# Branch products, output projection, second norm and the first up-projection steps written into one fixed order with the mLSTM

## The chip, the core and the metric

The kernel runs on one core of one Trainium2 chip. Its time is the device time of one execution in microseconds; a kernel is run several times and the median is taken. A profile is one more execution, with the hardware profiler on.

## What is computed

One layer of a diffusion backbone over 1024 tokens of width 1024, with 256 context tokens before them. All arithmetic has the accuracy of float32.

```
h   = modulate(rms_norm(x), sh1, sc1)               # six modulation rows from c
q, k, v, mq, mk, mv, mo, mg, ga, gm = split(h @ w_in)
att = windowed_gqa(q, k, v, context keys)           # 16 heads, window 128
ml  = mlstm_readout(mlstm_bidirectional(mq, mk, mv, mg), mo)
y   = sigmoid(ga) * (att @ w_branch_att) + sigmoid(gm) * (ml @ w_branch_ml)
x   = x + g1 * (y @ w_out)
u   = modulate(rms_norm(x), sh2, sc2) @ w_up        # 1024 -> 2 x 2816
out = x + g2 * ((silu(conv(u)_g) * conv(u)_a) @ w_down)
```

## The kernel before

**Products.** TensorE multiplies float32 operands as two parts: a high part, rounded on ScalarE (`copy_act`, L44), and a low part, the remainder, from VectorE (L49). One step of a product is three matmuls, high by high, low by high and high by low (`mm3`, L90 to L92; `product`, L1901 to L1903); most have 512 columns. A 1024 x 1024 x 1024 product is 16 tiles (one PSUM bank each) of 8 steps, 384 matmuls.

**Stages.** After the start come attention (about 90 to 645 us of the profile), the mLSTM (to about 1005), `stage_tail` (to about 1320) and `stage_ffn`. In attention and in the mLSTM every instruction of TensorE, VectorE, ScalarE and GpSimd is pinned behind the one before it on its engine (class `Pinned`, L494; all of these have line L504 in the trace). Their order is a string in which each letter is one small step: `ORDER` is run through once for each of the blocks of 128 tokens, `ORDER_GATES` and `ORDER_CORE` once. In `stage_tail` nothing is pinned: the program states the steps, and a scheduler places them on the engines.

**Around the change.** The last part of `ORDER_CORE` holds the first half of the attention branch product (letters N load, X high, Z low, Y step, l gate; tiles `ya`, operands `a0`, `a1`, `a2`, each 512 wide). Their buffers lie over the normalised input `hT`, which is closed when the mLSTM's output gate (`mo`) no longer needs it. `stage_tail` then has the second half of that product (`ya` on `wba1`), the mLSTM branch (`ym` on `mT`, `wbm0`, `wbm1`), the output projection (`op` on `y`, `wo0`, `wo1`), the second norm with its transposes (`x2t`), and the up projection, a product in fast form (seven products of half the size in place of eight): operands `b11`, `b21`, `t1` to `t4`, `b22` come from sums of quarters, and the weight sums of the down projection lie between projection tiles. The transposes of the pair sums (`x2p`) are stated between the last projection tiles.

**Modulation.** A modulation row of 512 is eight products on VectorE (`mod_product`, tiles `wmb` and `macc`) and then eight one-column matmuls over two rows (`mod_row`); `g1` and `g2` are transposed (`gT`) and stored. Products 0 to 47 are in attention (letter p of `ORDER`), 48 to 63 in the mLSTM branch of the tail, with three buffers.

**Memory and queues.** PSUM has 8 banks of 512 columns: two for products (`mm`), one (`fl`), three for transposes (`tp`) and two that attention uses for scores, the mLSTM for states (`d`) and the up projection afterwards. Each pool hands out its banks as they come free. Stored gates `sga_d`, `sgm_d` and first branch results `y1_d` are loaded over ScalarE's DMA queue (`ahead`), four tiles ahead; everything else is on SP's queue.

Of the kernel before, what the change touches and what calls it, by code (L numbers as in the profile page):

```python
# [99 lines left out]
def layer_kernel(ctx: ExitStack, tc: tile.TileContext, A: dict, out: bass.AP, dbg=None):  # L100
# [25 lines left out]
    ps1 = psx.enter_context(tc.tile_pool(name="ps_mm", bufs=2, space=PSUM, reuse_waits="tile"))  # L126
    pst = psx.enter_context(tc.tile_pool(name="ps_tp", bufs=3, space=PSUM, reuse_waits="tile"))
# [10 lines left out]
    def mm_tile(name):  # L138
        return ps1.tile([P, 512], F32, tag="mm", name=name)

    def fl_tile(name):
        return ps1.tile([P, 512], F32, tag="fl", name=name, bufs=1)

    def tp_tile(name):
        return pst.tile([P, 512], F32, tag="tp", name=name)

    def s_tile(name):
# [6 lines left out]
        nc=nc, tc=tc, A=A, ident=ident, expo=expo, vecT=vecT, mods=mods, m2=m2, g_d=g_d, wmod={}, maccs={}, rows=[], hT=hT, gtile=gtile, gb=gb, dr=dr, out=out,  # L154
        attT_d=attT_d, mlT_d=mlT_d, sga_d=sga_d, sgm_d=sgm_d, kx_d=kx_d, vx_d=vx_d, sil3=sil, sil=sil[:, :, 0], dbg=dbg,
        mm_tile=mm_tile, fl_tile=fl_tile, tp_tile=tp_tile, s_tile=s_tile, psx_s=psx_s,
# [21 lines left out]
    E.ph1, E.sX = ph1, ExitStack()  # L178
    with ExitStack() as st:
        stage_mlstm(E, st)  # L180
    if "mlT" in dbg:
        dump(nc, tc, mlT_d, dbg["mlT"])
# [6 lines left out]
    E.sX.close()  # L189
# [11 lines left out]
def mod_product(E, pool, n):  # L201
# [4 lines left out]
    if k == 0:  # L206
        E.macc = pool.tile([P, 512], F32, tag="macc", name=f"macc{i}", bufs=1 if q < 3 else 2)
        E.maccs[i] = E.macc
    ws, bufs = E.wmod, 1 if q < 3 else 3
# [9 lines left out]
    if k == KT - 1 and q < 3:  # L219
        E.rows.append(i)  # L220


def mod_row(E, pool, i):
# [294 lines left out]
def stage_attention(E, st, at):  # L518
# [306 lines left out]
    for n in range(N + 6):  # L825
        a, s, c, x, y = [Bs.get(n - d) for d in (0, 1, 3, 4, 5)]
        quota = (0, 0, 4)[n] if n < 3 else (7 if n < N else 10)
        for step in ORDER if n < N else ORDER_END:
# [37 lines left out]
            elif step == "p" and n < N and mods.n < 3 * (n + 1) // 2:  # L866
                mods.step()
# [18 lines left out]
    "vEvvvEvevvUvUvuEvuKvVveEwvvvUKAvuvVvBAvevwBqqKVqeqwwqwAqkkBHDDHmcUqzUqAzqcQuquyqqBqqqqSSQSSymmsmmsmhmmhSaSMSaSEmmsmmsh"  # L886
    "EmDeDammUcmUcmh1mumCu1mMaEmCmdemdmmEmDMDemcUmcUmumCmumCdOeIdOmmfmmMgmGmmDFIDcUmfmcUmMumCgmCmOdFIdOumfmmgmmMmFImDfDmcUm"
    "gUmCmcmFmMdOCuIAuOdmfmBmmAmgmvMBDFGIDUcvfcUvCuvCgvAvdFOdIBODfDuUvgUvAcvFcKIVuvCuvfwvCdvgvdvFBvvKvVvwvOIO1vf1vgvviIvKrv"
    "fvpVDgDvUiUvRvcvwvCcvuKdOVIuCO1wvfd1vgvviIvrvfpvgDDKVvUiUvRvcvwCcvuvCdvuOdIO1vf1xvgKvVviIwvrvfpvgvvivRKvVvwAOIO1xBvf1v"
    "AgvvivBIrqKfpqVqgAqRqwBqTiTwtqPwrqrPqrqprqtqpRQqApqyqRpRqBPkQkRPmHmyTHzPmmtzmTPSStSSSSsSSsmhmsmhmamMmhsmEmamhmamEmaemm"  # L890
    "mEDDmcmcUmMmUemuEmummmMmemDDmcUemcUmu1mum1mCmMmdGmmmDDmcUmCUmuMmdCmcmOdIMuOCmfmdmgmmmDFIDcUmfmcUCmgmMmCdOAFIuOdmfBmmAm"
    "gmvMBDGFIDUcvfUcvCuvCgvAvdFOuIBODfDdUvgUvAcvFcIKVvuCuvfwvCdvgvvdFvuBvKvVOwIOvfvgvvFIvfvDgDKVvUcUvwFvCcvuCvdOuIdO1vf1vg"
    "vviKIVvfwvDgDvUiUvcvcvCuCvudOIKdVO1vfw1vgvviIvfvDgDvUiUvcvcKvVuvCuCwvdOIdO1vf1xvgvviIvKVvfwvAgvviAOBIO1xvfB1vvgqKiVqwI"
    "rPqwrwqprqrpqARkpfmRmrBmprmDRrpDRqHgpqAqipQzTrTRUqtRUqRtpyqPcqRqcPuquBqPkQTPTHyStSSzStmmsSSsShSmhammsmMEmsmhmamhmameED"
    "aDmcmUmcmUmu1mMum1CmECmdmMmdemEDDmcemcmUmUmumCuOMIdGOmmmmmmfDCDgMmUmeUmcmFdIcmmuOummfmCmgMmCmDdFIdOUcDfmumUCgmmmdmMFcI"
    "OAummfmBCmmAmgvMDBGDFIUOcUvdvcvfuvuAgvCDBDCFIOUdfUvcvgAvdvKFVcICOuvfwCvdvgvdvFuIBvfvKvgVvwOFIO1vf1vgvviIvrvfpDKDVgvUvi"
    "UvRvcvwCcvuOCdIO1uvfd1vgKvVviIwvrvfpDDgvUviUvRvcKvcVuvCwCOdIO1dvfuvgvviIvrvfpvKVgvvivRvwvvOIKVOvfwvgvAviIvABvrvBfvpqgK"
    "VqRqwqiqrPqApTrTBkrPDrRDqpctcqHpqRtzqpQRqUyqURqPuuqPqqPkQTTHyStSSzStmmsSSsShSmhammsmNmsDhDamUhmUcmMNmcmCumCamDdDNmUcmU"
    "amnCmdMINdOOfcmnumCgImbmufDFdDumUcmbUmgOMmCcmFIdOCumfumdDDgmUmUcmFIcOMumfumCmgCmDdDFIcOUdmfUmcCmgmCmmMdFIuOdmfmnuDgDnm"
    "UcmUIcFOCumfumnCdmbmgnmMDbdDFIcUOcmfmuCmgCmbmmdbFIdOMmfDDgmmmimcIOcCmmfdCNgXXNiIMZNOXZfNZXYNgXYXNiYXZNIXOdYNfZXYZNXYgY"  # L900
    "NXiYXZIOZNYXZfYNZXYNgYNiYXZINXOZYfNZYXngYXYniXZIOXZYfZYbgYbYiIZrYZrYNplrYNlrpYfRYprlrYRprgYXYpRXYRpiYZrTpZTNtYpRtYNRRY"
    "RYZYXZTXZTYtlYtZYYYlYYYYYYYYlYYYYYYYYlYYYYYYYl"
# [3 lines left out]
def stage_mlstm(E, st):  # L906
# [5 lines left out]
    psd = E.psx_s.enter_context(tc.tile_pool(name="ps_d", bufs=2, space=PSUM, reuse_waits="tile"))  # L912
# [11 lines left out]
    zz = mp.tile([P, P], F32, name="zz")  # L924
# [1373 lines left out]
```

## Time and profile before

| | |
|---|---|
| time, median of 3 runs (lowest, highest) | 1936.34 us (1936.18, 1937.99) |
| time of the profiled execution | 1932.65 us |
| span of its profile | 1930.6 us |
| mean granted TensorE clock | 0.999 |
| TensorE busy | 99% |
| VectorE, ScalarE, GpSimd busy | 70%, 50%, 18% |
| DMA | 273.34 MB, mean 142 GB/s |

The span runs from the first to the last instruction in the profile; the profiled execution's time is 2 us longer, and the median of the runs without a profile 0.2% above that. Busy shares are averages over stages with different limits. A matmul's end is modelled, and matmuls overlap, so that the distance from one start to the next says more of TensorE's pace than a duration does.

### The profile page before, as it was taken

What the parts mean: (1) busy time and instruction counts of PE and PEld (TensorE: products, weight loads), DVE (VectorE), ACT (ScalarE), POOL (GpSimd) and SP (SyncE); (2) the same over time, 40 slices, a digit from 0 to 9 for tenths busy, and PEclk for the clock granted to TensorE, in tenths of its full rate; (3) what the DMA queues carried; (4) which work ended last, traced back from release to release, by engine and by line L of the source; (5) the groups of instructions that cost most, each with busy time, mean ns of one, the idle gap of its engine ahead of it and who ended that gap; (6) DMA issues with size and microseconds to landing.
All of it is one profiled execution on the core that took longest, in us unless ns stands there. A gap on an engine that the chain in (4) does not pass through costs nothing.

```text
span 1930.6 us, 28360 instructions
## 1 busy us (share of the span) xinstructions
PE 1902.0 (99%) x10108; PEld 1644.5 (85%) x10108; DVE 1352.8 (70%) x2642; ACT 963.4 (50%) x1897; POOL 346.9 (18%) x594
## 2 busy tenths in 40 slices
PE   8999999999999999999999999999999999999998
PEld 3988888888888899999997787887888888888887
DVE  2877767777776456666585467369878898895564
ACT  4856556556556354646354322256545444465441
POOL 1333333333333133434321000010000000000000
PEclk9999999999999999999999999999999999999999
DMA  8723223223222321413238667622244544499641
GB/s 313 231 93 94 77 66 104 72 77 91 80 67 74 103 62 51 117 49 99 55 122 277 219 201 238 231 88 81 94 151 187 196 153 174 164 326 326 230 164 66
DMA packets 134062, 273.34 MB, mean 142 GB/s; under 512 B 14736, under 2 KB 47136, under 8 KB 130592
## 3 DMA queue, kind: packets, MB, share of 16 engines
q1 hardware_dynamic: 127392, 256.85, 40.1%
q10 hardware_dynamic: 5760, 10.49, 1.7%
q0 software_dynamic: 768, 4.20, 1.3%
q8 instruction: 79, 1.29, 0.3%
q14 instruction: 63, 0.52, 0.1%
HBM read 201.67 MB, written 74.00 MB: 143 GB/s over the span
## 4 chain that ended last, share of the span: by engine, by line
PE 89%; DVE 4%; DMA 3%; ACT 2%; issue 1%; POOL 1%; SPq 0%; ACTq 0%; POOLq 0%; DVEq 0%
PE g L504 9%; PE kv L504 7%; PE pq L504 6%; PE mo L504 5%; PE pa L1901 4%; PE pa L1902 4%; PE pa L1903 4%; PE s L504 4%; PE po L504 4%; PE pt L504 3%; PE q L504 2%; PE ya L504 2%; PE dx L1901 2%; PE dx L1903 2%; PE dx L1902 2%; PE pb L1901 2%
## 5 line engine op out<-in xcount | busy, mean ns | idle before, releaser
L504 DVE CUSTOM_DVE_ANT_0 P<-s,maskA,nsink 128x640 f32<-128x640 f32 (+1 forms) x112 | 103.5, 924 | 76.8 <-PE s L504 75.2
L504 ACT ACTIVATE P<-P,st 128x640 f32<-128x640 f32 (+1 forms) x128 | 102.4, 800 | 87.9 <-DVE st L504 87.8
L504 ACT ACTIVATE ph<-pt 128x512 fp32r<-128x512 f32 x152 | 90.4, 598 | 60.0 <-PE pt L504 58.4
L504 DVE TENSOR_TENSOR pl<-pt,ph 128x512 fp32r<-128x512 f32 x152 | 101.1, 681 | 25.8 <-ACT ph L504 25.6
L504 POOL TENSOR_SCALAR P<-P,st 128x640 f32<-128x640 f32 (+1 forms) x128 | 110.9, 886 | 32.0 <-DVE st L504 11.1
L504 PE MATMUL g<-hH,fh 128*128 128x512 f32 x256 | 106.5, 416 | 0.2 <-ACT fo L504 0.2
L504 PE MATMUL g<-hH,fl 128*128 128x512 f32 x256 | 100.9, 394 | 0.0
L504 PE MATMUL g<-hL,fh 128*128 128x512 f32 x256 | 100.8, 394 | 0.0
L504 PE MATMUL pt<-ident,P 128*128 128x128 f32 x608 | 90.9, 272 | 0.5 <-DVE m L504 0.5
L504 PE MATMUL pq<-w1h,hH 128*128 128x384 f32 (+1 forms) x256 | 87.1, 340 | 0.0
L504 PE MATMUL kv<-w1h,hH 128*128 128x384 f32 x256 | 86.9, 340 | 0.0
L504 PE MATMUL pq<-w1l,hH 128*128 128x384 f32 (+1 forms) x256 | 86.9, 339 | 0.0
L504 PE MATMUL pq<-w1h,hL 128*128 128x384 f32 (+1 forms) x256 | 86.5, 338 | 0.0
L504 PE MATMUL kv<-w1h,hL 128*128 128x384 f32 x256 | 86.1, 336 | 0.0
L504 PE MATMUL kv<-w1l,hH 128*128 128x384 f32 x256 | 86.1, 336 | 0.0
L504 PEld LDWEIGHTS pt<-ident,P 128*128 128x128 f32 x608 | 75.4, 140 | 12.2 <-DVE m L504 0.7
L504 PE MATMUL mo<-w1h,hH 128*128 128x256 f32 x256 | 72.5, 283 | 0.0
L504 POOL TENSOR_SCALAR ss<-ss 128x5 f32<-128x5 f32 x64 | 13.2, 206 | 327.1 <-DVE ss L504 324.1
L504 PE MATMUL mo<-w1h,hL 128*128 128x256 f32 x256 | 71.8, 281 | 0.0
L504 PE MATMUL mo<-w1l,hH 128*128 128x256 f32 x256 | 71.7, 280 | 0.0
L49 DVE TENSOR_TENSOR dfl<-drf,dfh 128x512 fp32r<-128x512 f32 x55 | 38.0, 691 | 46.1 <-ACT dfh L44 46.1
L2039 ACT ACTIVATE cv<-ua,vecT 128x1024 f32<-128x1024 f32 x22 | 27.4, 1245 | 85.5 <-DVE ua L2012 85.5
(581 smaller groups left out, 6346.6 us busy)
## 6 DMA issues: line engine op xcount, KB each, us to landing
ur<-in_w_up SPq DMA_DIRECT2D x22, 1024.0 KB, 5.0
wmb<-in_w_modB SPq DMA_DIRECT2D x64, 256.0 KB, 2.8
f_d<-cv SPq DMA_DIRECT2D x22, 512.0 KB, 2.7
wm<-in_w_modA SPq DMA_DIRECT2D x16, 512.0 KB, 8.2
fr<-in_w_g SPq DMA_DIRECT2D x32, 256.0 KB, 2.7
drf<-fs_d SPq DMA_DIRECT2D x15, 512.0 KB, 5.8
drw<-wt_d SPq DMA_DIRECT2D x14, 512.0 KB, 5.6
w1b<-in_w_cx SPq DMA_DIRECT2D x16, 388.0 KB, 5.1
```

Of the source, the lines that this page charges most:

```text
L49: (nc.vector if eng == "v" else nc.gpsimd).tensor_tensor(lo, src, hi.bitcast(F32), op=ALU.subtract)
L504: i = f(*a, **k)
L1901: nc.tensor.matmul(ps, lh, rh, start=start and i == 0, stop=False, skip_group_check=True)
L1902: nc.tensor.matmul(ps, lh, rl, start=False, stop=False, skip_group_check=True)
L1903: nc.tensor.matmul(ps, ll, rh, start=False, stop=stop and i == n - 1, skip_group_check=True)
L2039: nc.scalar.activation(r, u, AF.Identity, bias=vecT[:, V_CB + ch : V_CB + ch + 1], scale=cw(1))
```

## The change

Everything from the first half of the attention branch to the first steps of the up projection is written out as small steps in one order, pinned on their engines like the mLSTM's.

- `ORDER_CORE` is rewritten. It keeps the mLSTM's letters and ends with 46 steps of the attention branch (Y). A new `ORDER_MERGE` follows: 82 steps Y, 128 of the mLSTM branch (`μ`), 128 of the output projection (`π`), all loads (2, 6, 8, <, 0, [), splits (X, Z, { }), gates (7, l, 9, @), the weight sums (]), the squares and powers of the second norm (o, W), its scaling, transposes and affine steps (Greek letters) and the first two tiles' steps of the up projection (`ι`).
- Operands are [128, 1024] and lie in 40 numbered slots (class `Gen`): 24 over `hT`, the rest in two pools that are closed before the second norm. A slot is given back after the last step that reads it. High parts are written 1024 wide on ScalarE, low parts 1024 wide on VectorE.
- The products' tile order changes: tokens are walked so that each weight half serves both token halves (`tiles`, `mtiles`).
- Gates and first branch results are loaded over SP's queue, in four buffers each.
- PSUM banks are fixed: a ring over banks 0 and 1, bank 2, a ring over 3 to 5, and one over 6 and 7.
- All 64 modulation products are in attention, two for each p-step until they are done, with one buffer; the tail has none.
- `stage_tail` starts with the transposed and scaled first half given, and states the pair sums (`pair_sums(0, ..)` with its transposes), `t1`, `t3`, the second half and the units of the up projection. The transposes of the pair sums stand behind the projection.
- The 1024-wide operand buffers of the FFN are 4 on one side of SBUF and 6 on the other, in fixed rotation; the FFN's `xm` tiles use the buffers of `acc`.

The core of the diff:

```diff
-    ps1 = psx.enter_context(tc.tile_pool(name="ps_mm", bufs=2, ...))
-    pst = psx.enter_context(tc.tile_pool(name="ps_tp", bufs=3, ...))
+    mm_tile, tp_tile, c_tile = ring("mm", 0, 2), ring("tp", 3, 3), ring("d", 6, 2)
...
-            elif step == "p" and n < N and mods.n < 3 * (n + 1) // 2:
+            elif step == "p" and n < N and mods.n < min(2 * (n + 1), 64):
...
-    for m in range(n, min(n + bufs, 48 if q < 3 else 64)):
-        if m not in ws:
-            ws[m] = pool.tile([P, 512], F32, tag="wmod", name=f"wmb{m}", bufs=bufs)
-            nc.sync.dma_start(ws[m], E.A["w_modB"][m // KT][:, m % KT])
-    w = ws.pop(n)
+    w = pool.tile([P, 512], F32, tag="wmod", name=f"wmb{n}", bufs=1)
+    nc.sync.dma_start(w, E.A["w_modB"][n // KT][:, n % KT])
...
     for c in ORDER_CORE:
-        next(gens[c])
+        if c in gens:
+            next(gens[c])
+        else:
+            merge[c].pop(0)()
...
+class Gen:
+    def __init__(self):
+        self.free, self.of, self.left, self.top = list(range(24)), {}, {}, 40
...
+    def tile(self, key, name, dt=F32R, lim=40):
+        i = self.of[key] = next(i for i in self.free if i < lim)
+        self.free.remove(i)
+        return self.pools[(i >= 24) + (i >= 32)].tile([P, 1024], dt, tag=f"g{i}", name=name)
...
+    def used(self, key):
+        self.left[key] -= 1
+        if self.left[key] == 0:
+            i = self.of.pop(key)
+            if i < self.top:
+                self.free.append(i)
...
+def merge_steps(E, cols, mm3_step):
...
+    def load(key, src, scale=None):
...
+            T[key] = gs.tile(key, nm(key)).bitcast(F32)
+            nc.sync.dma_start(k2(T[key]), src)
...
+    def split(key, src, last, lim=40, ys=False):
+        def high():
+            h = gs.tile((key, "h"), nm(key) + "h", F32R, lim)
+            T[key] = h, gs.tile((key, "l"), nm(key) + "l", F32R, lim)
+            act.activation(h, T[src], AF.Copy)
+
+        def low():
+            dve.tensor_tensor(T[key][1], T[src], T[key][0].bitcast(F32), op=ALU.subtract)
...
+    def gate(src, n, t, c, key):
+        def ld():
+            open_early()
+            sg[key] = E.sgp.tile([P, 512], F32, tag="sg", name=f"sg{key}")
+            rs, ts = place(n, t, c)
+            nc.sync.dma_start(sg[key], src[rs, ts])
...
+    def turned(k):
+        pt[k] = E.tp_tile(f"x2t{k}")
+        for c in C4:
+            pe.transpose(pt[k][:, c * P : (c + 1) * P], xs[c][:, k * P : (k + 1) * P], E.ident)
...
+def merges_rest(E):
...
+    for c in ORDER_MERGE:
+        E.merge[c].pop(0)()
...
-        project(1, b, w)
-        square(b)
...
-    U.lead(0)
     U.prep_apart(0, lambda n, dt=F32R: x512(n, dt, 1))
     scale(5)
-    first_half(H)
-    project(1, 6, w)
-    square(6)
     fa = [op2(f"fa{k}", F32) for k in range(H)]
     for k in range(H):
         pair_sums(0, k, fa[k])
     scale(6)
-    project(1, 7, w)
-    square(7)
     put_t1(0)
     for k in range(H):
         t3(0, k)
-    U.lead(1)
-    U.first_mm(0)
+    U.mid[0] = E.first[0], E.first[1]
     scale(7)
```

## Rows read from the trace of the kernel before

**Rows 1.** The page: TensorE's busy time and the chain that ended last.

```profile
PE 1902.0 (99%) x10108; PEld 1644.5 (85%) x10108; DVE 1352.8 (70%) x2642; ACT 963.4 (50%) x1897; POOL 346.9 (18%) x594
...
PE 89%; DVE 4%; DMA 3%; ACT 2%; issue 1%; POOL 1%; SPq 0%; ACTq 0%; POOLq 0%; DVEq 0%
```

**Rows 2.** Busy time in windows.

```profile
core 0: us, PE busy (x) PEld busy (x) DVE busy (x) ACT busy (x) POOL busy (x), PEclk, DMA share, GB/s
1000.00:1350.00 350.00, 340.46 (x1555) 278.44 (x1554) 221.77 (x374) 143.38 (x267) 18.27 (x32) 1.00 0.56 191
1175.00:1200.00 25.00, 21.50 (x90) 16.93 (x88) 19.72 (x30) 5.49 (x7) 0.00 (x0) 0.93 0.74 243
1400.00:1450.00 50.00, 50.00 (x223) 41.38 (x222) 39.55 (x48) 22.74 (x27) 0.00 (x0) 1.00 0.45 161
```

**Rows 3.** Tiles ya, ym, op on TensorE: min/median/max ns, first and last start.

```profile
L90 PE MATMUL ya<-a1h,wba1h x32: 387/389/395, 1055.7 to 1079.3; 128*128 128x512 f32 x32
...
L90 PE MATMUL ya<-a2h,wba1h x32: 389/389/389, 1080.0 to 1101.1; 128*128 128x512 f32 x32
...
L90 PE MATMUL ym<-mTh,wbm0h x64: 389/389/497, 1101.8 to 1145.6; 128*128 128x512 f32 x64
...
L90 PE MATMUL ym<-mTh,wbm1h x64: 389/389/632, 1146.3 to 1195.3; 128*128 128x512 f32 x64
...
L90 PE MATMUL op<-wo0h,yh x64: 389/389/504, 1196.8 to 1242.5; 128*128 128x512 f32 x64
...
L90 PE MATMUL op<-wo1h,yh x64: 389/389/476, 1243.2 to 1292.0; 128*128 128x512 f32 x64
```

**Rows 4.** Timeline of TensorE around the end of the projection: start, us.

```profile
1285.32 1.47 PE L1791 MATMUL x2p<-ident,acc 128*128 128x128 f32 x12
...
1292.73 0.39 PE L1901 MATMUL pa<-b11h,r1h 128*128 128x512 f32 x1
...
1318.13 0.39 PE L1901 MATMUL pa<-b11h,r1h 128*128 128x512 f32 x1
...
1321.98 0.39 PE L1903 MATMUL pa<-b11h,r1l 128*128 128x512 f32 x1
```

**Rows 5.** Waits of TensorE, 1000 to 1350 us: sum, times, longest.

```profile
PE ym L90 <- DVE sgm L1711: 2.7, 2, 2.4
...
PE gT L234 <- DVE m L229: 1.6, 1, 1.6
```

**Rows 6.** Timeline of TensorE, mLSTM branch, second half.

```profile
1183.33 0.50 PE L90 MATMUL ym<-mTh,wbm1h 128*128 128x512 f32 x1 [2.36 <-DVE sgm L1711]
```

**Rows 7.** Groups of instructions by form, 1000 to 1350 us.

```profile
L49 DVE TENSOR_TENSOR wbm1l<-wbm1r,wbm1h 128x1024 fp32r<-128x1024 f32 x4 | 4.9, 1223 | 2.6 <-ACT wbm1h L44 2.6
...
L44 ACT ACTIVATE wbm1h<-wbm1r 128x1024 fp32r<-128x1024 f32 x4 | 4.2, 1053 | 2.9 <-DMA wbm1r<-in_w_bm 2.1 <-DVE yl L49 0.8
```

**Rows 8.** DMA issues, 1000 to 1350 us: KB each, us from issue to landing.

```profile
y<-y_d ACTq DMA_DIRECT2D x16, 256.0 KB, 4.3
...
wba1r<-in_w_ba SPq DMA_DIRECT2D x4, 512.0 KB, 5.3
```

**Rows 9.** Timeline of TensorE, end of the mLSTM and first branch steps.

```profile
1000.69 0.28 PE L504 MATMUL mo<-w1h,hL 128*128 128x256 f32 x1
...
1005.45 0.51 PE L504 MATMUL ya<-a1h,a0h 128*128 128x512 f32 x1 [0.18 <-ACT a1h L504]
1006.87 0.50 PE L504 MATMUL ya<-a1l,a0h 128*128 128x512 f32 x1 [0.92 <-DVE a1l L504]
```

**Rows 10.** Timeline of SP's queue in the same place.

```profile
1001.01 0.33 SPq L1504 DMA_DIRECT2D ar<-in_w_ba  x1
```

**Rows 11.** Timeline of VectorE, pair sums to the last low half of t4.

```profile
1286.56 0.43 DVE L1784 TENSOR_TENSOR acc<-fa,acc 128x256 f32<-128x256 f32 x1 [0.34 <-ACT fa L1768]
...
1320.20 0.69 DVE L49 TENSOR_TENSOR t4l<-acc,t4h 128x512 fp32r<-128x512 f32 x1
```

**Rows 12.** Waits of VectorE, 100 to 640 us.

```profile
DVE P L504 <- PE s L504: 83.8, 87, 2.8
```

**Rows 13.** Tile wmb: min/median/max ns, first and last start.

```profile
L504 DVE SCALAR_TENSOR_TENSOR macc<-wmb,sil,macc x42: 741/745/753, 108.0 to 582.3; 128x512 f32<-128x512 f32 x42
```

**Rows 14.** Waits of SP's queue, 1000 to 1350 us.

```profile
SPq L1740 <- DVE acc L1738: 47.0, 8, 7.7
```

More of the change, by code (lines that the diff above doesn't have):

```diff
@@ L188, in layer_kernel @@
         stage_tail(E, st)
-    E.sX.close()
+    E.sA.close()
+    psx_s.close()
     psx.close()
@@ L890 @@
[L890 to L893, printed above, removed]
@@ L1544, in att_step @@
[L1544 to L1558 removed]
+    E.bk = bk
@@ new lines, in merges_rest @@
+def merges_rest(E):
+    nc, tc, gs = E.nc, E.tc, E.gen
+    E.y1s = ExitStack()
+    E.y1p = E.y1s.enter_context(tc.tile_pool(name="y1t", bufs=4, side="right", reuse_waits="tile"))
+    left = lambda name, bufs: E.sX.enter_context(tc.tile_pool(name=name, bufs=bufs, reuse_waits="tile"))
+    E.g1p, E.g1b = left("g1t", 1), None
+    vecT, m2, V_N2 = E.vecT, E.m2, 24
+    nc.vector.scalar_tensor_tensor(m2[:, 2], m2[:, 2], 1.0, vecT[:, V_N2 : V_N2 + KT], op0=ALU.add, op1=ALU.mult)
+    nc.vector.tensor_scalar(m2[:, 2], m2[:, 2], float(D) ** 0.5, None, op0=ALU.mult)
+    E.s2, E.s3 = ExitStack(), ExitStack()
+    gs.pools.append(E.s3.enter_context(tc.tile_pool(name="gb", bufs=1, reuse_waits="tile")))
+    gs.pools.append(E.s2.enter_context(tc.tile_pool(name="gc", bufs=1, reuse_waits="tile")))
+    gs.free += [*range(28, 40), *range(24, 28)]
+    for c in ORDER_MERGE:
+        E.merge[c].pop(0)()
+    assert not any(E.merge.values())
+    E.sX.close()
@@ L1634, in x512 @@
         return xts[pool].tile([P, 512], dt, tag="x", name=name)
-    g1b = tp1.tile([P, D], F32, name="g1b")
     g2b = tp1.tile([P, D], F32, name="g2b")
-    m2 = E.m2[:, 1:3]
-    tiles = [(n, t, c) for n in range(2) for t in range(2) for c in range(4)]
-    def place(i):
-        n, t, c = tiles[i]
-        r0 = n * 512 + c * P
-        return slice(r0, r0 + P), slice(t * 512, (t + 1) * 512)
-    def ahead(pool, src, tag, nm, bufs, first=0):
-        got, todo = {}, list(range(first, 16))
-        def take(i):
-            while todo and todo[0] <= i + 3:
-                j = todo.pop(0)
-                got[j] = pool.tile([P, 512], F32, tag=tag, name=f"{nm}{j}", bufs=bufs)
-                rs, ts = place(j)
-                nc.scalar.dma_start(got[j], src[rs, ts])
-            return got.get(i)
-        return take
@@ L1677, in stage_tail @@
-    for q in range(4):
-        ml_load(q)
-    for i, (n, t, c) in list(enumerate(tiles))[8:]:
-        sg = gate(i)
-        ps = mm_tile(f"ya{i}")
-        mm3(nc, ps, w, aT[t], sl(c * P, P), sl(0, 512))
-        ac = nc.scalar.activation(sg, sg, AF.Sigmoid)
-        dv = nc.vector.tensor_tensor(sg, ps, sg, op=ALU.mult)
-        rs, ts = place(i)
-        sto = nc.sync.dma_start(y1_d[rs, ts], sg)
-        with tc.issue_after(ac.ins), tc.issue_after(dv.ins), tc.issue_after(sto.ins):
-            for q in (2 * i - 16, 2 * i - 15):
-                ml_split(q)
-                ml_load(q + 4)
-        if i == 11:
-            with tc.issue_after(sto.ins):
-                wm = load_w(A["w_bm"][0], "wbm0")
```

602 lines of the change are left out of this document (369 added, 233 removed).

## Prediction

> **What bounds the kernel now.** I read the page first: TensorE is busy 99% of a span of 1930.6 us at the full clock, and the chain that ended last lies on it for 89% [rows 1]. So a change of order can only win back what TensorE loses between matmuls, and the first question is how much that is in the stretch that is reordered.
>
> I then cut the span into windows. In a late up-projection stretch TensorE shows no idle time; from 1000 to 1350 us, which holds the two branch products, the output projection, the second norm and the start of the up projection, it is busy 340.46 of 350 us [rows 2]. That looks like 9.5 us to win. But the end of a matmul is modelled, so I measured by starts instead. Four tiles of one branch product are 96 matmuls of 512 columns. The ones in the fourth row group start at 1080.0 and the next product at 1101.8: 21.8 us, 0.227 us each, with nothing lost [rows 3]. Against that pace, 192 matmuls should take 43.6 us, and each group's excess is its loss:
>
> - second weight half of the attention branch, first tokens, 1055.7 to 1080.0: 24.3 - 21.8 = 2.5;
> - mLSTM branch, first half, 1101.8 to 1146.3: 44.5 - 43.6 = 0.9;
> - mLSTM branch, second half, 1146.3 to 1196.8: 50.5 - 43.6 = 6.9, of which two sets of eight one-column matmuls of the modulation rows are about 1.6 (they move, and are paid elsewhere), so 5.3;
> - output projection, first half, 1196.8 to 1243.2: 46.4 - 43.6 = 2.8;
> - output projection, second half, 1243.2 to 1292.73, where the first up-projection matmul starts [rows 4]: 49.5 - 43.6 = 5.9, less 48 transposes that lie among it at (1.47 - 0.27) / 11 = 0.11 each, from twelve of them in one run [rows 4] (5.2): 0.7.
>
> That is 12.2 us. The view of TensorE's waits names the causes: PSUM banks that VectorE had not emptied (ym, 2.7 us in two waits) and the transposed gate row in the middle of the work (gT, 1.6) [rows 5]. The waits sum to less than the loss, because a long one costs more than itself. After the 2.36 us wait at 1183.33 [rows 6] the granted clock of that window of 25 us is 0.93 [rows 2]: the clock fell from its 2.4 GHz level to 1.2 GHz, which takes 0.07 x 25 = 1.75 us.
>
> A sentence of the Trainium skill fits here: its page Perfetto Trace Analysis, section Identifying the Most-Contended Engine, says that matmul busy time is no good measure of headroom and the busy share of weight loads is. The rows agree: weight loads are busy 278.44 of 350 us here and 41.38 of 50 at full pace [rows 2], so 278.44 us are the work of 278.44 / 0.828 = 336.4, and 13.6 are missing. By busy time alone the stretch would have 4.1 us less to give, and the sum below would be -2.2 and end at 1934.
>
> **The change, part by part.** The matmuls stay the same in number and shape: 384 steps of three for the two branches and the projection, the same transposes, the same up products. So does the work on VectorE and ScalarE, except that operands are split 1024 wide. So every term is a loss of TensorE that goes, stays or appears.
>
> *Middle, 12.2 us now.* The new order writes out 128 steps for each product and puts each operand's load, high half and low half between them. I counted steps at 0.68 us (3 x 0.227). From the middle of the mLSTM branch on, almost every operand's low half stands 18 to 37 us ahead of its first use; only the second weight half of the attention branch (3 us) and two merged-token operands (1.3 us) are close. A 1024-wide split costs 1.05 us on ScalarE and 1.22 on VectorE [rows 7], and a 512 KB load lands in 5.3 us [rows 8]; the closest case with a load has 8.1 us from load to use, and the sum is 7.6. VectorE has about 119 us of work against 239 us of steps, ScalarE 79. The transposed gate row leaves this stretch. So the middle should lose little: I take 1.0 us, between 0 and the 6 that would remain if half of the waits came back. Gain 11.2.
>
> *The junction to the mLSTM.* The first operands now lie in slots over the normalised input, so their loads start when the last gate step has read it. Before shows that this release is immediate: the last matmul of the gate step ran from 1000.69 to 1000.97 [rows 9], and a load into the freed place was issued at 1001.01 [rows 10]. From that read to the first branch step the new order has 7 gate steps and 14 state and output steps, 7 x 0.354 + 14 x 0.36 = 7.5 us. The chain is issue 0.3, load 5.3, two high halves 2.1, one low half 1.22, some 0.2 of signals: 9.1. Stall 1.6 us. Before loses 1.5 there (some 0.3 and 1.2 beyond pace at the starts 1005.45 and 1006.87, with the waits shown there [rows 9]). Cost 0.1, from -1.5 to +3 if four loads at once slow each other.
>
> *The tail after the projection.* This is the part that gives back. Before, the transposes of the pair sums ran between projection tiles: they begin at 1285.32 [rows 4], VectorE starts on them at 1286.56, and is then occupied up to the end of the last low half of the last operand (t4) at 1320.89 [rows 11], 34.3 us. So VectorE had a lead of 6 us on the end of the projection. From 1292.73 to 1321.98 [rows 4], 29.25 us, TensorE issued 108 matmuls of the first two units (24.5), 16 transposes (1.7) and five of the third unit (1.1): it lost 1.9. In the new order these transposes stand in the tail, behind the last of the 128 projection steps and 24 up-projection matmuls (5.45 us). VectorE's work is 34.3 less what now comes earlier (one add 0.6, two scalings 1.4, one weight split 1.1) = 31.2. It starts 5.45 + 1.24 = 6.7 us after the last projection step and ends at 37.9; the last matmuls follow at 38.6. TensorE has 108 matmuls and 32 transposes in that time, 28.0 us, and 24 of the third unit (5.45) that it can pull in as before did. So it loses 5.2 us, 3.3 more than now. Bounds: 1.9 (if transposes are again placed earlier) and 10.6 (if nothing is pulled in). I take 5.2, because the matmul on r1 at 1318.13 belongs to the third unit and ran ahead of the last ones on t4 [rows 4].
>
> *Attention.* Sixteen modulation products move here: 16 x 0.745 = 11.9 us on VectorE, which waits 83.8 us there for scores [rows 12]; the 0.745 is from [rows 13]. In every second block the pattern of two per block exists already. Hidden: 0.5, at most 4 if half of them delayed a score. Their 16 loads go on SP's queue, which has three a block now. Two more modulation rows and one more gate row come with them; a gate row's transpose can wait up to the 1.6 us of [rows 5]: 1.0. Cost 1.5, from 0.5 to 5. In the mLSTM the order is new, but TensorE keeps pace there; a loss is bounded by what the attention order loses, and I take none.
>
> *Sum:* -11.2 + 0.1 + 3.3 + 1.5 = -6.3 us. The profiled execution took 1932.65 us with a span of 1930.6, so its span becomes 1924.3 and its time 1926.4; the median of the runs is 1936.34, 0.2% above, and the forecast for it is **1930 us**. A difference below 0.2% (3.9 us) is about what cannot be told from none.
>
> **The rivals.**
>
> *The tail stays covered (1926.7).* If the pair transposes are placed between the last projection steps, the 3.3 us vanish: 1926.7; with a clean middle too, 1923 or so. For it: before's planner did place later work between steps. Against it: the projection steps now come first in the program and are almost always ready.
>
> *The tail is bare (1935.4).* Nothing fills it: loss 10.6 in place of 5.2, 5.4 more. Then the middle's gain is mostly given back within 40 us. For it: VectorE has those 34.3 us without a pause and no second start [rows 11]. It decides if the third unit's split, which stands before the last operands on VectorE, comes after them.
>
> *Slower: loads behind stores on SP (1942).* Gates and first-branch results came over ScalarE's own queue (40 loads of 256 KB, 4.3 us each [rows 8]); now all go through SP, where a store waits for its VectorE result, up to 7.7 us in the projection [rows 14]. A gate load behind such a store is 7.7 + 4.3 = 12 us late, beyond the 10.9 that two free PSUM banks (two tiles of 5.45) cover; ScalarE then holds every split behind that sigmoid. One such hold costs about 4.3 and the fallen clock about 1.75 more [rows 2]: 6. Two of them cancel the forecast gain, and it decides at two. Against it: loads have buffers 20 us ahead. The Trainium skill (TensorE: Matmul & The Clock Gate, Architectural detail) says that ScalarE and VectorE take instructions strictly in order, which is what makes one late load stop a whole order; the waits in [rows 5] agree.
>
> *No effect (1936).* The same waits come back at other tiles, because VectorE and ScalarE do the same work.
>
> **How the numbers follow.** Forecast 1930 (own range 1927 to 1932.5): 0.45. Covered tail: 0.17. Bare tail: 0.20. Slower: 0.13. No effect: 0.05. Faster is 0.45 + 0.17 = 0.62, same 0.20 + 0.05 = 0.25, slower 0.13. The range takes in the covered tail with a clean middle (1923) and the near side of the slower case (1941).
>
> **What would show it.** Right: between the first branch step and the last projection step TensorE's starts keep 0.227 us, no wait on ym or gT and no fallen clock; a stall of 1 to 2 us at the first branch step; the pair transposes after the last projection step, VectorE solid for 30 us and about 5 us of gaps there. Wrong: several gaps over 2 us in the middle that end on a DMA; gaps in the mLSTM; or a tail that loses 10 us.

## The result and the profile after

The changed kernel takes 1943.32 us, the median of 14 runs (1936.29 to 1947.14), and the kernel before 1936.32 us in 14 runs beside them: a ratio of 1.0035, 95% interval 1.0024 to 1.0045. It is slower by some 7 us; 1930 was forecast. The profiled span is 1940.2 us, 9.6 more than before.

The page of the changed kernel, busy time and the chain that ended last:

```profile
PE 1907.6 (98%) x10108; PEld 1649.8 (85%) x10108; DVE 1347.4 (69%) x2611; ACT 966.4 (50%) x1870; POOL 344.1 (18%) x594
...
PE 92%; DVE 3%; DMA 2%; ACT 1%; issue 1%; POOL 1%; SPq 0%; ACTq 0%; DVEq 0%; POOLq 0%
```

TensorE has the same 10108 matmuls and still bounds the kernel. So I compared when it reaches the same points. Tiles ya, ym and op of the changed kernel (min/median/max ns, first and last start), and its timeline at the ends of the projection and of operand t4:

```profile
L516 PE MATMUL ya<-pa_a_0h,pa_w_0h x32: 389/389/796, 1011.9 to 1110.7; 128*128 128x512 f32 x32
...
L516 PE MATMUL ym<-pm_m_0h,pm_w_0h x32: 389/389/389, 1115.4 to 1197.7; 128*128 128x512 f32 x32
...
L516 PE MATMUL op<-o_pB_0h,o_pA_0h x64: 387/389/477, 1202.5 to 1291.3; 128*128 128x512 f32 x64
```

```profile
1293.31 0.39 PE L516 MATMUL pa<-b11h,r1h 128*128 128x512 f32 x1
...
1310.65 0.50 PE L2091 MATMUL pa<-t2h,q11h 128*128 128x512 f32 x1 [2.36 <-ACT ua L44]
...
1321.13 0.80 PE L2093 MATMUL pa<-t3h,q2l 128*128 128x512 f32 x1 [2.47 <-DVE q2l L49]
...
1333.86 0.39 PE L2093 MATMUL pa<-b11h,r1l 128*128 128x512 f32 x1
```

Against [rows 3, 4, 9] the changed kernel is behind by

| point | before | after | behind |
|---|---|---|---|
| first branch step | 1005.45 | 1011.9 | 6.5 |
| mLSTM branch | 1101.8 | 1115.4 | 13.6 |
| output projection | 1196.8 | 1202.5 | 5.7 |
| up projection | 1292.73 | 1293.31 | 0.6 |
| after the last step on t4 | 1321.98 | 1333.86 | 11.9 |
| end | 1930.6 | 1940.2 | 9.6 |

It loses 6.5 us before the branches and 7.1 in the attention branch, wins 13.0 in the mLSTM branch and the projection, and loses 11.3 again after the projection. Some of this is work that only moved:

- sixteen transposes (1.7 us), from the projection to behind it;
- sixteen one-column matmuls of two modulation rows (1.6 us), from the mLSTM branch to attention;
- twelve matmuls of the mLSTM (tiles i and o, 0.12 us each, 1.4 in all), which now stand behind the first branch step;
- five matmuls of the third unit (1.1 us): by the last step on t4 the changed kernel has done ten of them, before five.

Like for like the changed kernel loses 6.5 - 1.6 + 1.4 = 6.3 us before the branches. From there to the end of the projection it wins (1292.73 - 1005.45) - (1293.31 - 1011.9) - 1.7 - 1.6 + 1.4 = 4.0 us, and behind it it loses 11.3 - 1.7 - 1.1 = 8.5 us. The windows tell the same, before and then after (columns as in [rows 2]):

```profile
100.00:150.00 50.00, 47.63 (x262) 43.36 (x261) 37.03 (x101) 24.94 (x61) 18.80 (x28) 1.00 0.27 86
...
800.00:900.00 100.00, 100.00 (x710) 97.63 (x709) 66.03 (x185) 54.88 (x131) 36.48 (x81) 1.00 0.26 68
...
1050.00:1100.00 50.00, 48.03 (x211) 39.04 (x210) 19.55 (x26) 14.69 (x22) 0.00 (x0) 1.00 0.72 248
1100.00:1293.00 193.00, 187.91 (x844) 153.14 (x843) 114.34 (x172) 63.38 (x113) 6.50 (x14) 0.99 0.56 194
1293.00:1350.00 57.00, 55.61 (x250) 44.89 (x249) 53.88 (x96) 37.69 (x71) 3.35 (x2) 1.00 0.25 84
```

```profile
100.00:150.00 50.00, 46.75 (x252) 42.35 (x251) 37.01 (x101) 24.02 (x59) 16.75 (x26) 0.97 0.30 97
...
800.00:900.00 100.00, 98.20 (x687) 95.15 (x686) 64.28 (x177) 52.68 (x130) 37.69 (x83) 1.00 0.26 68
...
1050.00:1100.00 50.00, 45.32 (x191) 36.56 (x190) 17.31 (x18) 17.70 (x22) 0.00 (x0) 0.93 0.88 292
1100.00:1293.00 193.00, 193.00 (x868) 159.89 (x867) 95.69 (x122) 57.22 (x90) 6.35 (x14) 1.00 0.53 182
1293.00:1350.00 57.00, 51.69 (x225) 40.54 (x224) 52.42 (x105) 39.45 (x79) 1.47 (x2) 0.94 0.24 80
```

From 1100 to 1293 us TensorE is now busy for all of 193.00 us: no loss is left there. How much of that the order itself has won is a question for the runs of the kernel before with small parts of the change. Idle time and fallen clock stand on both sides of it. The fallen clock counts as busy: 0.93 over 50 us is another 3.5 us.

Four places, then: near 108 us, in the mLSTM, before the second weight half of the attention branch, and after the projection. I tried each by itself. In what follows "us" beside a ratio is the difference of the ratios times 1936, and the changed kernel stands at 1.0035 throughout. Both ratios have an interval, so a difference between two variants is uncertain by some 3 us or more.

### The profile page after: what moved, and what is told of

Read it like the earlier page. It is cut to its first block, busy times and chain, and to the rows that moved or that the text cites. A ratio compares the mean times of both kernels' runs of the same rounds, so it can differ in the third digit from the quotient of the medians.

```text
span 1940.2 us, 28322 instructions
## 1 busy us (share of the span) xinstructions
PE 1907.6 (98%) x10108; PEld 1649.8 (85%) x10108; DVE 1347.4 (69%) x2611; ACT 966.4 (50%) x1870; POOL 344.1 (18%) x594
## 4 chain that ended last, share of the span: by engine, by line
PE 92%; DVE 3%; DMA 2%; ACT 1%; issue 1%; POOL 1%; SPq 0%; ACTq 0%; DVEq 0%; POOLq 0%
PE g L516 9%; PE kv L516 7%; PE pq L516 6%; PE op L516 5%; PE ym L516 4%; PE ya L516 4%; PE pa L2093 4%; PE pa L2091 4%; PE pa L2092 4%; PE mo L516 4%; PE s L516 4%; PE po L516 3%; PE pt L516 3%; PE q L516 2%; PE pb L2092 2%; PE pb L2093 2%
## 5 line engine op out<-in xcount | busy, mean ns | idle before, releaser
L516 PE MATMUL pq<-w1h,hL 128*128 128x384 f32 (+1 forms) x256 | 87.1, 340 | 0.0
L49 DVE TENSOR_TENSOR dfl<-drf,dfh 128x512 fp32r<-128x512 f32 x55 | 37.9, 691 | 48.6 <-ACT dfh L44 48.5
L44 ACT ACTIVATE dfh<-drf 128x512 fp32r<-128x512 f32 x55 | 34.5, 630 | 68.3 <-PE dy L2092 34.4
```

The source lines that it names most:

```text
L44: nc.scalar.activation(out, in_, AF.Copy, scale=scale)
L49: (nc.vector if eng == "v" else nc.gpsimd).tensor_tensor(lo, src, hi.bitcast(F32), op=ALU.subtract)
L516: i = f(*a, **k)
```

## Experiments on the tail

**Pair sums in the fixed order.** The scaling of rows 4 and 5, four sets of transposes, their affine steps and twelve subtractions become steps of the order:

```diff
-    "...θππ^πoππWππππ^ππoπππππι^ιoWιι"
+    "...θππaa^πboπbcWπdbcπdbcππdcdπ^ππoπππππι^ιoWιι"
+    op("a", pair_scale); op("b", pair_turn); op("c", pair_affine); op("d", pair_sub)      # abridged: one for each row or k
```

Their tiles lie in buffers of gates and of the first gate row, which are free by then; the FFN's 512-wide operands share the four gate buffers in place of four of their own.

> The changed kernel, with the scaling of token rows 4 and 5, the first four pair transposes, their affine steps and their twelve subtractions written into the fixed order before the last projection tile. Theory (the tail is late because VectorE gets its first pair sum only at 1300 us of the profile, after idling through the projection): about 5 us of VectorE work and 1.7 us of transposes leave the tail, its loss on TensorE falls from 10.3 us to between 4 and 6, and the time falls by 4 to 6 us, to about 1938. Rival (the tail is bound by the 30 us of other splits, whatever starts them): under 1.5 us. Second rival (the scaling waits for the store of its row, and the transposes then hold TensorE inside the projection): no gain, with a new wait of 1 to 3 us before the transposes.

Measured: 0.9997 of before (0.9987 to 1.0006), 7.4 us below the changed kernel. ScalarE and VectorE of the changed kernel, then VectorE of this one:

```profile
1299.39 1.93 ACT L1999 ACTIVATE fa<-x2p,m 128x256 f32<-128x256 f32 x4 [3.20 <-PE x2p L2013]
...
1310.02 0.58 ACT L44 ACTIVATE ua<-pa 128x512 f32<-128x512 f32 x1
```

```profile
1297.97 0.75 DVE L1986 TENSOR_SCALAR acc<-acc,mods 128x1024 f32<-128x1024 f32 x1
1299.99 0.42 DVE L2006 TENSOR_TENSOR acc<-fa,acc 128x256 f32<-128x256 f32 x1 [1.26 <-ACT fa L1999]
...
1331.04 0.68 DVE L49 TENSOR_TENSOR t4l<-acc,t4h 128x512 fp32r<-128x512 f32 x1
```

```profile
1283.90 0.43 DVE L517 TENSOR_TENSOR acc<-fa,acc 128x256 f32<-128x256 f32 x1 [2.39 <-ACT fa L517]
...
1322.51 0.68 DVE L49 TENSOR_TENSOR t4l<-acc,t4h 128x512 fp32r<-128x512 f32 x1
```

The first subtraction moves from 6.7 us after the projection (1299.99 - 1293.31) to 9.5 before it, and the last low half comes 8.5 us sooner. The windows of this kernel show 55.29 us busy from 1293 to 1350 at a clock of 1.00, in place of 51.69 at 0.94; before has 55.61. So the late start of the pair sums was nearly all of the tail's extra loss. It was late on two engines, which the edit moves together: the affine steps on ScalarE start 6.1 us after the projection, and TensorE's first stop, 2.36 us at 1310.65, ends on ScalarE's copy of `ua` behind them; only the second, 2.47 us at 1321.13, ends on VectorE. No run moves one of the two alone.

**First up tile later.** The 24 matmuls leave the fixed order and stand behind the first pair sums:

```diff
-    U.mid[0] = E.first[0], E.first[1]
+    U.first_mm(0)
```

> The changed kernel, with the first up-projection unit's first 24 matmuls taken out of the fixed order and stated behind the first pair sums in the tail. Theory A (TensorE's order is what is late): the transposes follow the last projection matmul, 5.45 us earlier, and the time falls by about 5 us. Theory B (VectorE is what is late; it is occupied with the second unit's weight sums from 1294.1 to 1298.7 anyway): the first subtraction starts only about 1.3 us earlier, the loss falls from 10.3 to about 9 us and the time by about 1 us.

Measured: 1.0018 (1.0009 to 1.0027), 3.3 us below the changed kernel, between the two theories. The transposes start at 1293.53, VectorE's first subtraction at 1294.93, 5.1 us earlier than in the changed kernel: the scheduler put the second unit's sums between the pair sums, where theory B had them ahead. It did not move the start to before the projection's end, and 3.3 us are about the uncertainty of a difference.

## Experiments on the gates and their queue

The wait before the second weight half, on the timelines of SP's queue, ScalarE and TensorE of the changed kernel:

```profile
1056.47 0.95 SPq L1494 DMA_DIRECT2D mlT_d<-mo  x2
1057.52 0.40 SPq L1704 DMA_DIRECT2D y_d<-sga  x1
...
1062.46 0.32 SPq L1693 DMA_DIRECT2D sga<-sga_d  x1
1062.88 1.18 SPq L1601 DMA_DIRECT2D a_w<-in_w_ba  x2
```

```profile
1055.08 0.63 ACT L516 ACTIVATE sga<-sga 128x512 f32<-128x512 f32 x1 [4.61 <-issue]
1055.76 1.32 ACT L516 ACTIVATE mo<-mt,mlw 128x512 f32<-128x512 f32 x2
...
1067.16 0.63 ACT L516 ACTIVATE sga<-sga 128x512 f32<-128x512 f32 x1 [9.22 <-DMA sga<-sga_d]
1067.69 1.04 ACT L516 ACTIVATE pa_w_0h<-a_w 128x1024 fp32r<-128x1024 f32 x1
```

```profile
1063.76 0.39 PE L516 MATMUL ya<-pa_a_3h,pa_w_3l 128*128 128x512 f32 x1
1068.79 0.80 PE L516 MATMUL ya<-pa_a_0h,pa_w_0h 128*128 128x512 f32 x1 [4.64 <-ACT pa_w_0h L516]
...
1071.49 0.63 PE L516 MATMUL ya<-pa_a_0h,pa_w_0l 128*128 128x512 f32 x1
1071.92 0.63 PE L516 MATMUL ya<-pa_a_1h,pa_w_1h 128*128 128x512 f32 x1
```

And of the waits of SP's queue, 1036 to 1075 us:

```profile
SPq L1693 <- DMA y_d<-sga: 11.0, 5, 5.8
```

Read it backwards. TensorE waits for the copy of the weight, which stands on ScalarE behind a sigmoid, which waits 9.22 us for its gate. That load was issued at 1062.46 only, some 5 us after the store of 1057.52: there are four gate buffers, a branch result is written into the buffer of its gate, and the next load into it waits until the result is stored. The store itself came late, behind two stores of `mo`, which wait for ScalarE, which had stood 4.61 us before a sigmoid. For this last wait the row names no releaser ("issue"); the run with the new buffers first has the same 4.61 us there, and it ends on a gate's load. After the wait matmuls start 0.43 us apart: the clock is at its lower level. The Trainium skill (TensorE: Matmul & The Clock Gate, Architectural detail) has ScalarE work strictly in order; the two ScalarE rows at 1067 agree. In six further runs with the gates on this queue and four buffers for them the wait before the second weight half is 2.6 to 5.2 us, so its length differs from run to run.

**More gate buffers.** Four more from the start of the second string on, used in turn with the old ones:

```diff
-            sg[key] = E.sgp.tile([P, 512], F32, tag="sg", name=f"sg{key}")
+            E.sgn += 1
+            sg[key] = (E.sgq if E.sgq and E.sgn % 2 else E.sgp).tile(...)
```

> The changed kernel, with four more buffers for gates from the start of the second order string on; queue and order stay. Theory (a gate's load waits until the branch result in the same buffer is stored, and the weight loads behind it on SP's queue and the weight copies behind its sigmoid on ScalarE wait with it): the wait of 4.6 us before the second weight half of the attention branch goes, with the fallen clock behind it 5 to 7 us, to about 1937. Rival (SP's queue is late because stores wait in it for VectorE and ScalarE): the wait stays above 3 us.

Measured: 1.0026 (1.0017 to 1.0035), 1.7 us below the changed kernel, which is less than the uncertainty. The wait for the first weight copy is 0.9 us, below all of those, but four waits of 2.9 us in all are left (0.9, 1.0, 0.5, 0.5); SP's queue still waited for a branch result's store six times, 7.5 us at most: half of the loads still fell to the old buffers.

**The new buffers first.** The same buffers, in another turn:

```diff
-            E.sgn += 1
-            sg[key] = (E.sgq if E.sgq and E.sgn % 2 else E.sgp).tile(...)
+            E.sgn += E.sgq is not None
+            sg[key] = (E.sgq if E.sgq and (E.sgn - 1) // 4 % 2 == 0 else E.sgp).tile(...)
```

> The changed kernel with the same four further gate buffers as in the run with more gate buffers, but the first four gate loads of the second order string all go to them, then four to the old ones, and so on. Theory (the wait before the second weight half comes from a gate load that waits for the store of the branch result in its buffer): no gate load near 1050 to 1063 us waits for a store any more, the four waits of 0.5 to 1.0 us that were left there shrink to below 1.5 us in sum, and the time is 5 to 7 us below the changed kernel, at 1.000 to 1.001 of before. Rival (the weight loads are late by SP's order and by DMA throughput): the waits stay near 3 us in sum and the time near that of the first buffer run, 1.0026 of before.

Measured: 1.0018 (1.0009 to 1.0027), 3.3 us below the changed kernel. Waits of TensorE, 1000 to 1100 us, and of SP's queue, 1036 to 1075 us, in this kernel:

```profile
PE ya L516 <- DVE pa_a_0l L516: 1.4, 1, 1.4
PE ya L516 <- ACT pa_w_0h L516: 1.2, 1, 1.2
PE ya L516 <- DVE pa_w_1l L516: 0.5, 1, 0.5
PE ya L516 <- DVE pa_w_0l L516: 0.5, 1, 0.5
```

```profile
SPq L1706 <- DVE sga L516: 12.5, 5, 6.8
SPq L1494 <- ACT mo L516: 4.6, 3, 4.1
SPq L1695 <- DMA y_d<-sga: 3.3, 3, 2.0
```

Three waits for the second weight half remain, 2.2 us, and three loads of gates still wait for a store. So both theories hold in part: with more buffers the long wait goes, but the gain is 3.3 us where 5 to 7 was expected. What keeps the weight loads late is read from the rows, not tested: three of the four are issued at 1056.05 only, behind a store of `mo` that waited 4.1 us for ScalarE, and from issue to landing they take 6.7 us in the median, where 512 KB took 5.3 in [rows 8]. The longest wait, 6.8 us of a store for VectorE, stands behind them.

**Loads on ScalarE's queue.**

```diff
-            nc.sync.dma_start(sg[key], src[rs, ts])
+            act.dma_start(sg[key], src[rs, ts])
...
-            nc.sync.dma_start(y1[key], E.y1_d[rs, ts])
+            act.dma_start(y1[key], E.y1_d[rs, ts])
```

> The changed kernel, with the loads of gates and of first branch results issued on ScalarE's queue at the same places of the order. Theory (buffers): a gate's load now waits on ScalarE for the store of its buffer and holds the copies behind it, so the wait before the second weight half stays within 2 us of 4.6, or grows. Rival (order of SP's queue): the weight loads no longer stand behind gates, the wait falls below 2 us and the time by 4 us or more.

Measured: 1.0099 (1.0082 to 1.0116), 12 us above the changed kernel. The wait at the second weight half did fall to 1.4 us, as the rival had it, but new ones came. Waits of TensorE, 1000 to 1293 us, and of ScalarE, 1000 to 1200 us:

```profile
PE ym L516 <- DVE sgm L516: 6.4, 3, 3.6
PE mt L516 <- ACT mo L516: 2.5, 1, 2.5
```

```profile
ACT sgm L516 <- DMA sgm<-sgm_d: 47.2, 9, 8.1
```

In a fixed order a load that waits on ScalarE's queue holds ScalarE, as the theory had it, only at other tiles.

**The same part in the kernel before**, in `ahead`:

```diff
-                nc.scalar.dma_start(got[j], src[rs, ts])
+                nc.sync.dma_start(got[j], src[rs, ts])
```

> The kernel before with this part of the change alone: gates and first branch results loaded over SP's queue in place of ScalarE's. Theory (a load on SP's queue stands behind stores that wait for VectorE): 2 to 8 us slower, with waits of TensorE on ym or ya that end on VectorE or ScalarE. Rival (the scheduler's places are early enough): within 1 us.

Measured: 0.9967 of before (0.9955 to 0.9979), 6.4 us faster. The theory, which was my slower rival, falls: SP's queue was the better place for these loads in both kernels.

## Experiments on the modulation and the mLSTM's order

**All modulation products early, in the kernel before**, with one buffer:

```diff
-            elif step == "p" and n < N and mods.n < 3 * (n + 1) // 2:
+            elif step == "p" and n < N and mods.n < min(2 * (n + 1), 64):
...
-            for _ in range(2 if i in (2, 9) else 1 if i < 14 else 0):
-                mod_product(E, mp, made)
-                made += 1
-        if i in (9, 15):
-            mod_row(E, mp, 6 + i // 15)
```

> The kernel before with this part of the change alone: all 64 modulation products in attention, one buffer, two in each block, none in the mLSTM branch. Theory (attention pays 1 to 4 us, the mLSTM branch gets back the waits on its banks and the two rows, 2 to 5 us): between 0 and 3 us faster than before. Rival (free in attention): 4 to 6 us faster.

Measured: 0.9960 (0.9949 to 0.9972), 7.7 us faster than before, more than either theory said; its interval, 5.4 to 9.9 us, takes in the upper end of the rival's.

**Both in the kernel before**, the two diffs together.

> The kernel before with two parts of the change: all modulation products in attention, and gates and first branch results loaded over SP's queue. Theory (both parts end the same loss, the 2.4 us wait near 1183 us and the fallen clock, so they do not add up): 7 to 9 us below before, 0.9955 to 0.9965. Rival (two separate gains): 12 to 14 us below before, 0.993 to 0.994.

Measured: 0.9965 (0.9953 to 0.9977); they don't add up. Their common term is [rows 6]. VectorE of before, there:

```profile
1181.99 0.69 DVE L1784 TENSOR_TENSOR w<-w,w 128x512 f32<-128x512 f32 x1 [2.40 <-DMA w<-in_w_dn]
1182.60 0.68 DVE L1711 TENSOR_TENSOR sgm<-ym,sgm 128x512 f32<-128x512 f32 x1
```

The PSUM bank was full because VectorE stood 2.40 us at a weight sum of the down projection whose load was late. With either part the view of TensorE's waits from 1100 to 1293 us has no wait on a bank of ym any more. That each ends this wait is shown; how is not. A late load alone can't be it: in the kernel with all products early VectorE stands even longer for these loads from 1100 to 1293 us, where before has 5.8 us in four waits:

```profile
DVE w L1778 <- DMA w<-in_w_dn: 11.7, 6, 3.7
```

The sums stand at other places in both kernels, which may be what counts.

From 1100 to 1293 us TensorE is busy 191.27 us with all products early, 191.51 with the loads on SP's queue and 191.60 with both, where before has 187.91 and the changed kernel 193.00. The changed kernel holds both parts, so of the 5.1 us of idle time that it wins there, 3.7 come without the long order as well, and 1.4 are left for the order. No run takes the two parts out of the changed kernel.

What the products cost in attention is not shown. From 100 to 150 us before has 47.63 us busy at a clock of 1.00; before with all products early, and then the changed kernel with the first up tile later, which has the same products there:

```profile
100.00:150.00 50.00, 47.67 (x259) 43.74 (x258) 36.97 (x101) 24.35 (x58) 16.70 (x26) 0.97 0.30 98
```

```profile
100.00:150.00 50.00, 46.93 (x264) 42.66 (x263) 37.46 (x102) 24.76 (x58) 16.97 (x26) 1.00 0.31 98
```

In the first, 0.03 x 50 = 1.5 us went to the clock, the figure that was forecast for attention. But the clock is 1.00 in the second and in two more runs with all products early, so it can't be taken as the price of the products. From 100 to 640 us TensorE is busy 536.05 us with all products early and 535.43 before.

**Sixteen products left out of the changed kernel:**

```diff
-            elif step == "p" and n < N and mods.n < min(2 * (n + 1), 64):
+            elif step == "p" and n < N and mods.n < min(3 * (n + 1) // 2, 48):
...
-    for i in E.rows:
+    E.maccs[6] = E.maccs[7] = E.maccs[5]
+    for i in E.rows + [6, 7]:
         mod_row(E, dp, i)
```

> The changed kernel with the old rate of modulation products in attention, three in two blocks; the last 16 products are left out and their two rows are formed from the last sum before them, so that the second gate of the output differs. Theory (the 16 extra products and their loads cost 1 to 4 us in attention): the loss between 90 and 300 us falls from about 11 us to about 8 us, the time by 1.5 to 4 us. Rival (they are hidden behind waits for scores): within 1 us.

Measured: 1.0061 (1.0041 to 1.008), slower by 5 us. Neither theory. At the old rate the rows fall at other places of a block, and TensorE's transposes wait there; waits from 130 to 640 us:

```profile
PE pt L516 <- DVE pl L516: 3.8, 2, 2.0
```

So a part of an order can't be priced by leaving it out when the steps that are left then meet other waits.

**One product less in the first block**, made up in the second:

```diff
-            elif step == "p" and n < N and mods.n < min(2 * (n + 1), 64):
-                mods.step()
+            elif step == "p" and n < N and mods.n < min(2 * (n + 1), 64) - (n == 0):
+                mods.step()
+                if n == 1 and mods.n == 2:
+                    mods.step()
```

> The changed kernel with the second modulation product of the first attention block moved to the second block (three there, then two as before). Theory (that product stands on VectorE ahead of the work for the first turned queries; the wait for them grows from below 2.4 us to over that and the clock falls): the wait near 108 us is 2.0 to 2.4 us, the loss between 100 and 150 us falls from about 6 us to about 3.5, and the time by 1.5 to 3 us. Rival (the wait there is set by the start of the kernel, which differs from run to run): loss and time stay within 1 us.

Measured: 1.0036 (1.0021 to 1.0051), no change. TensorE waits for the first turned queries near 108 us and again some 10 us later. The first wait fell from 3.10 us to 1.93, as the theory had it, but the second grew from 0.16 to 3.17: the edit moved the product into the next block's way, so it does not tell theory from rival. In the changed kernel and eight variants with the same attention steps these waits sum to 2.5 to 3.8 us, and to 2.2 to 2.4 in the three kernels with the old rate of products. So the sum differs by over 1 us from run to run, as the rival says.

**Old order of the mLSTM:**

```diff
-for c in NEW_CORE:
+for c in OLD_CORE[:1500] + "".join(the steps of NEW_CORE that are not among them, in its order):    # in words; the string is written out
```

> The changed kernel, with the first 1500 steps of the mLSTM's order (all of it up to the first step of the attention branch in the old string) put back to the old order; the rest keeps the new one. Theory (the new order brings the scaled keys from GpSimd too late at two places near 800 and 894 us, which cost 0.6 to 1.4 us each and some clock): the losses there, 3.4 us between 800 and 900 us, fall to below 1 us as before, and the time by 2 to 3 us. Rival (GpSimd is slower in the changed kernel whatever the order): they stay.

Measured: 1.0020 (1.0011 to 1.0029), 2.9 us below the changed kernel; from 800 to 900 us TensorE is busy 99.90 us, where the changed kernel has 98.20. The theory holds. GpSimd in the changed kernel, and TensorE's step behind it:

```profile
798.41 2.53 POOL L516 TENSOR_TENSOR ub<-ub,mlmask 128x512 f32<-128x512 f32 x2 [1.36 <-DMA ub<-u_d]
800.93 0.72 POOL L516 TENSOR_SCALAR kwh<-k,gcall 128x128 fp32r<-128x128 f32 x2
```

```profile
801.35 0.39 PE L516 MATMUL dC<-VH,kwh 128*128 128x258 f32 x1 [0.60 <-POOL kwh L516]
```

The new order has two mask products, which had waited for their load, ahead of the scaled keys that TensorE needs next.

**Old bank pools.** The rings become pools with as many buffers:

```diff
-            return pst.tile([P, 512], F32, tag=f"tp{i}", name=name)      # bufs=1
+            return pst.tile([P, 512], F32, tag="tp", name=name)          # bufs=3, and so for mm and d
```

> The changed kernel with the PSUM banks in pools as before in place of the fixed rings. Theory (the rings cost nothing, since a pool also goes round its banks): within 1.5 us of the changed kernel. Rival (a ring makes a tile wait for one bank where another is free): 2 to 5 us faster than the changed kernel.

Measured: 1.0043 (1.0028 to 1.0058), not told apart from the changed kernel. Pools win nothing back, so the rings are no cause of the loss.

## Experiments with the parts together

**Changed kernel repaired**: pair sums early, new gate buffers first, old mLSTM order.

> The changed kernel with three parts together: pair sums of rows 4 and 5 in the fixed order before the last projection tile, the four further gate buffers used first, and the mLSTM's steps up to the first attention branch step in the old order. Theory (three separate losses that add up: 7, 3 to 5 and 2.5 us): 12 to 15 us below the changed kernel, 0.995 to 0.998 of before. Rival (one loss covers another; what is won ahead is lost in the tail): at or above 0.998 of before.

Measured: 0.9968 (0.9957 to 0.998), 13.0 us below the changed kernel; the single parts sum to 7.4 + 3.3 + 2.9 = 13.6. That is what three separate losses give, within the intervals. This kernel and the kernel before with either or both of its parts (0.9960 to 0.9967) all beat before; their intervals overlap.

**With the product of the first block moved**, the repaired kernel and the kernel before with both parts:

> The repaired kernel (pair sums early, more gate buffers, old mLSTM order) with that product moved too. Theory: another 1.5 to 3 us, 0.995 to 0.996 of before. Rival: the same as the repaired kernel, 0.997.

> The kernel before with the two parts (modulation early, loads over SP's queue) and that product moved too. Theory: another 1 to 2 us, about 0.9955 of before. Rival: the same as without, 0.9965.

Measured: 0.9981 (0.9971 to 0.999) and 0.9968 (0.9955 to 0.998): no gain in either.

## Why the prediction was wrong

The sum was -11.2 + 0.1 + 3.3 + 1.5 = -6.3; about +7 was measured, outside the range.

- *Middle, gain 11.2.* This term failed first: from the first branch step to the end of the projection 4.0 us were won, like for like. From the mLSTM branch to the last projection step it was right: 1202.5 - 1115.4 = 87.1 us for the mLSTM branch's 384 matmuls, 0.227 each, no loss at all. But I had counted the second weight half of the attention branch as close, 3 us ahead, and kept 1.0 us for the whole middle. The attention branch lost 13.6 - 6.5 = 7.1 us more than before, 5.7 without the twelve matmuls that moved there. I had checked the weights' own load, copy and low half against their distance, and the gates for their queue, not for their buffer: a store, a load and a sigmoid lie between two uses of it. The gate buffers give 3.3 us back; where the rest goes is not tested.
- *Tail, 3.3.* The mechanism was right, the size not: pair transposes behind 24 up matmuls, VectorE 6.7 us after the projection, as worked out there, occupied to 38.4 us behind it (1331.04 + 0.68 - 1293.31; 37.9 was forecast). The step that failed is the five us of the third unit's matmuls that I let TensorE pull in. At the steps on t2 and t3 it stopped twice, 2.36 and 2.47 us, and the third unit's matmuls came behind both stops: ten of the 24, where I had all. The stop at t2 ends on ScalarE, whose work in the tail I had not counted. By the prediction's count the loss is 1333.86 - 1293.31 = 40.6 us less 28.0 and 2.3 for the ten, 10.3 us: 8.4 more than before's 1.9, not 3.3. In the window from 1293 us it is 57 - 51.69 = 5.3 us idle and 0.06 x 57 = 3.4 of clock. The rival with the bare tail, a loss of 10.6, was the better one, in part by luck, since it has no fallen clock in it. Putting the work ahead won 7.4.
- *mLSTM, none.* Measured 2.9. I took "TensorE keeps pace there" from the old order and put no bound on what GpSimd's order could cost.
- *Junction, 0.1, and attention, 1.5.* The stall at the second branch step is 1.4 us, where 1.6 was worked out. Attention's 1.5 is not shown: a clock of 0.97 costs as much in some runs and does not appear in others with the same products. From 100 to 640 us the changed kernel has 0.4 us more idle time than before (534.99 us busy against 535.43). Of the 6.3 us lost before the branches, some 3.4 are not in the mLSTM's 2.9 and no run takes them apart; what sets the wait near 108 us stays open too.
- *The rivals.* "Slower, 1942" had the time by luck and part of the cause. One gate's load did come late, hold ScalarE's copies behind its sigmoid and let the clock fall, for about the 6 us that it gives to one such hold; there was one and not two, and the rest of the time came from the tail and the mLSTM. Its reason is the lesser one: SP's queue waited 11.0 us for stores of the gate buffers from 1036 to 1075 us and 7.7 us for VectorE. And SP's queue as such was a gain.
- *One unclear term:* the 1.6 us of the two modulation rows were taken out of the middle's loss as paid elsewhere. The 1.0 us in attention is said to be for these rows and a gate row, so that part of them may be charged without having been credited.

What I had not asked at all is whether the fixed order was needed for the gain. The main wait of the middle goes with the modulation products or with the queue alone, and 1.4 us of idle time from 1100 to 1293 us are left for the order.

## What to carry to other kernels

When an order is fixed, follow each buffer through its whole round (load, first use, last use, store, next load), not only each operand from load to use; everything behind the late load on its queue and on the engine that reads it is late too. Work of a side engine that the next stage needs must stand in the order before the end of this one: here the scheduler left it behind pinned steps that were always ready. Before writing out an order, try its small parts alone; here two edits of a few lines each gave as much as the long order with its faults mended.

## What was not expected of the hardware

Nearly equal waits left the granted clock at different levels. Near 108 us a wait of 2.27 us goes with a clock of 1.00 from 100 to 150 us in the run with the first up tile later, and with 0.97 in the kernel before with all products early; one of 2.88 us, in the run with the old mLSTM order, goes with 1.00. The two stops in the tail, 2.3 to 2.4 and 2.47 us, are in seven further runs: from 1293 to 1350 us the clock is 0.94 in four of them, as in the changed kernel, and 1.00 in three. There the fallen clock is worth 3.4 us, so one profile does not price such a stop.

In the attention branch the wait cost clock each time. Before the second weight half, waits of 4.3 to 5.2 us left 0.93 from 1050 to 1100 us in all four kernels that have them, the changed kernel among them, and waits of 2.6 to 3.2 us left 0.97 in three. In the changed kernel 8.2 us are lost in this window, 4.7 idle, nearly all of it the wait of 4.64, and 3.5 by the clock. By starts the clock took 3.0: the twelve matmuls from 1068.79 to 1074.48 needed 5.7 us, not 2.7. So this wait cost about two thirds more than itself.
